# Gating stage of a streaming encoder: u of tiles 0 and 1 by seven block products for six of eight groups instead of four

## The chip, the cores and the metric

The kernel runs on one core of one Trainium2 chip. The metric is the time of one execution on the device, in microseconds (us); 2098.18 us is the median of three runs before the change. Engines are named as in the profile: PE (TensorE, matmuls), PEld (its weight loads), DVE (VectorE), ACT (ScalarE), POOL (GpSimd) and SP (SyncE, which here issues the DMAs).

## The reference

A two-layer encoder step for 1024 prompt rows and 32 sample rows of width 1024, in fp32. Layer 0 mixes by spatial gating, layer 1 by pooling; each has a squared-ReLU FFN behind it. The change concerns the gating:

```python
def sgu_mixer(h, w_in, g_v, w_s, b_s, w_out, T):
    """gMLP spatial gating: u * (W_s v + b) within chunks of T positions (T <= 128)."""
    z = jax.nn.gelu(h @ w_in)                 # (rows, 4096)
    u, v = jnp.split(z, 2, axis=-1)           # 2048 each
    v = rmsnorm(v, g_v)
    vr = v.reshape(bsz, L // T, T, SGU_GROUPS, SGU_GROUP_DIM)      # 8 groups of 256
    w = w_s[:, :T, :T] * sgu_chunk_mask()[:T, :T]
    s = jnp.einsum('gij,bnjgd->bnigd', w, vr) + b_s...
    return (u * s) @ w_out, v                 # w_out: 2048 x 1024
...
x = x + gt1 * rmsnorm(mix, g_norm[i, 1])
h = rmsnorm(x, g_norm[i, 2]) * (1 + sc2) + sh2
f = jnp.square(jax.nn.relu(h @ ffn_w_up[i])) @ ffn_w_down[i]
```

The normalised v of the sample rows is an output too (`state_sgu_sample`).

## The kernel before

Activations lie feature-major (features on partitions, rows as columns), in three tiles: tile 0 and tile 1 of 384 prompt rows, tile 2 of 256 prompt and the 32 sample rows. Every fp32 matrix is kept as a high and a low part (`wh`, `wl`, `hh`, `hl`), and a product is three matmuls: high with high, high with low, low with high (`products`, L1134 to L1136). ACT makes the high part of a weight by a copy (L592), DVE the low part by a subtraction; all wrapped DVE operations, that one too, have line L80.

**Weights** come as a list `stream` of pieces of 512 KB, written out at the start of the program. SP loads them into three `raw` buffers in the order of the list; `stream_step`, called from `weave()` between the products, consumes them in that order. `some_ada(n)` puts n pieces of the adaLN weights into the list; these are multiplied on DVE, four steps of 128x512 a piece. `fillers` are generators for other work (sums, norms, the state output) that `weave()` advances when their turn comes. A scheduler then places each engine's instructions, so the order on an engine isn't that of the code.

**The gating stage** follows the v part. Its list `mixes` names pairs of groups and the tiles they are done for. `sgu_item` does one entry for one tile in the plain form: four blocks of u (128 features each, 24 matmuls into `pu`, gelu at L1600); per group the spatial product (`spatial`, L1531, tiles `psp`) from a load `vl` of the v rows (L1499); `gate` multiplies; `split` makes `ush` and `usl`; `down` adds eight blocks `po` to the tile's sum `acc`. `upairs()` does the groups in `UPAIRS` for tiles 0 and 1 together: `pair_item` with a `gate` computes u of two blocks of features for both tiles from 2x2 blocks by seven products of 12 matmuls (`quad_product`, L1758 to L1760, into `pfau`, `pfbu`, `pfcu`) instead of eight. For this `quads` forms the weight sums (A1, S31, S24, A22) on DVE, and the filler `u_sums` the sums of activations (`usum_*`, kept in `combo_u`, `combo_acc`, `combo_r` and, for one of the four, in the place of tile 0's first half, which must no longer be needed then). Its `hook` runs the spatial products and the gating between the seven products, `place` keeps the result, and the down half is 192 matmuls (`pgu`).

Before, the entries are: groups 4 and 5 of tile 0; 6 and 7 of tile 0; then `upairs()` for groups 0 to 3 of tiles 0 and 1; groups 0, 1 and 2, 3 of tile 2; then 4, 5 and 6, 7 of tiles 1 and 2. When a tile's sum is complete, its norm and residual (`to_ffn0`: `pn_r_0x` for tile 0, `pn_rs` for tile 1) go into the fillers, and the FFN of layer 0 follows (`pf`, `pg`, and in its own pair chunks `pfa`, `pfb`).

The filler `state` (`sgu_state`, L1421 to L1440) writes the sample's normalised v in four steps: loads of `vst` (L1426) and `gvb` (L1428, a row broadcast to 32 partitions), one DVE step, a store (L1439). Its two buffers, the `vl` loads and two of the places of a pair chunk come from one pool, `x3`, with three places.

Of the kernel before, what the change touches and what calls it, by code (L numbers as in the profile page):

```python
# [35 lines left out]
def tile_stream_encoder_step(  # L36
# [99 lines left out]
    def A(t, kb, c0=0, w=None):  # L136
        w = ncol[t] - c0 if w is None else w
        return acc[t][:, kb, HALO + c0 : HALO + c0 + w]
# [5 lines left out]
    def ps_up(name):  # L144
        return psum.tile([P, 512], F32, tag="pu", bufs=2, name=name)

    def ps_dn(name):
        return psum.tile([P, 512], F32, tag="pd", bufs=3, name=name)

    def ps_ms(name):  # L150
        return psum.tile([P, 512], F32, tag="pm", bufs=3, name=name)

    def t_m(name):
        return work.tile([P, 384], F32, tag="m", bufs=3, name=name)
# [4 lines left out]
    def t_hid(kind, name, dtype=F32R):  # L159
        return work.tile([P, 384], dtype, tag="h" + kind, bufs=5, name=name)  # L160
# [185 lines left out]
    def w_groups(n):  # L346
        gs, _ = mixes[n]
        for g in gs:
            for k in range(2):
                f = 2 * g + k  # L350
                add_w(
                    ("u", n, g, k),
                    sgu_w_in[0][:, f * P : (f + 1) * P].rearrange("(k p) f -> p k f", p=P),
                    (8, P),
                )
        for q in range(2):
            for g in gs:
                add_w(
                    ("o", n, g, q),
                    sgu_w_out[0][g * 256 : (g + 1) * 256, q * 512 : (q + 1) * 512].rearrange(  # L360
                        "(k p) d -> p k d", p=P
                    ),
                    (2, 512),
                )

    def w_upair(p):
        for j in range(4):
            f = 4 * p + j
            add_w(
                ("up", ("u", p), j),  # L370
                sgu_w_in[0][:, f * P : (f + 1) * P].rearrange("(k p) f -> p k f", p=P),
                (8, P),
                ("one", "two")[j % 2],
            )
        for q in range(4):
            add_w(
                ("dn", ("u", p), q),
                sgu_w_out[0][p * 512 : (p + 1) * 512, q * 256 : (q + 1) * 256].rearrange(
                    "(j p) d -> p j d", p=P
                ),  # L380
                (4, 256),
            )
# [31 lines left out]
    every = list(range(NT))  # L414
# [5 lines left out]
    passes += [(1, c, PAIR, 1) for c in range(1, 8)]  # L420
    passes += [(1, c, [NT - 1], 2) for c in (0, 2, 4, 6)]
    LEND_AT = (("v", 1, 3), ("up", 0, 0))
    UPAIRS = (0, 1)

    rest = []

    def some_ada(n):
        for _ in range(min(n, len(rest))):
            add, l, j = rest.pop(0)
            add(l, j)  # L430
# [20 lines left out]
        some_ada(8)  # L451
    rest += [(add_wide, 1, j) for j in (*range(8, 16), *range(8), *range(16, 48))]

    mixes = [((4, 5), every[:1]), ((6, 7), every[:1]), ((0, 1), every[2:]), ((2, 3), every[2:])]
    mixes += [((4, 5), every[1:]), ((6, 7), every[1:])]
    for n in range(len(mixes)):
        w_groups(n)
        if n == 1:
            for p in UPAIRS:
                w_upair(p)  # L460
                some_ada(3)
        if n > 3:
            some_ada(5)
    for n, (l, c, tiles, m) in enumerate(passes):
        if tiles == PAIR:
            w_chunk(n, (1 if c < 3 else 2) if l else (5 if c == 1 else 6) if c < 7 else 1)
# [360 lines left out]
    def need_w(key):  # L827
        state["used"] = max(state["used"], wpos[key])
        while key not in witem:
            assert stream_ready(), key  # L830
            stream_step()
        return witem[key]
# [8 lines left out]
    def w_finish(key):  # L841
        w_free(key)
# [35 lines left out]
    def weave(streams=1):  # L878
        if streams:
            n = 0  # L880
            run_deferred()
            while n < streams and stream_ready() and not stream_waits():
                turn = bool(subs) and stream[state["next"]][0] == "wide"
                stream_step()
                n += not turn
        while time["dve"] < time["pe"] - slack[0] and fillers:
            if not pull():
                break
# [240 lines left out]
    def products(ps, n, terms, of=None):  # L1129

        i0, last = (0, len(terms) - 1) if of is None else (of[0], of[1] - 1)
        tick(3 * len(terms) * (0.004 + n / 2265.0))
        for i, (wh, wl, rh, rl) in enumerate(terms, i0):
            mm(ps[:, :n], wh, rh, start=i == 0, stop=False)  # L1134
            mm(ps[:, :n], wh, rl, start=False, stop=False)  # L1135
            mm(ps[:, :n], wl, rh, start=False, stop=i == last)  # L1136
# [100 lines left out]
    with tc.manual_schedule():  # L1237
# [63 lines left out]
        ps = ps_ms("pv0_5")  # L1301
# [105 lines left out]
    for p, b in v_order:  # L1407
        ps = ps_dn(f"pv{p}_{b}")
# [40 lines left out]
    def flush():  # L1449
        while pending:  # L1450
            pending.pop(0)()

    def split(dst_hi, dst_lo, src, n):
        act(out=dst_hi[:, :n], in_=src[:, :n], func=AF.Copy)  # L1454
        tt(out=dst_lo[:, :n], in0=src[:, :n], in1=dst_hi[:, :n].bitcast(F32), op=ALU.subtract)

    def accumulate(t, d, ps, first):
        n = ncol[t]
        if first:
            act(out=A(t, d), in_=ps[:, :n], func=AF.Copy)  # L1460
        else:
            tt(out=A(t, d), in0=A(t, d), in1=ps[:, :n], op=ALU.add)

    def up_terms(wkey, t):
        wh, wl = need_w(wkey)
        return [
            (wh[:, k * P : (k + 1) * P], wl[:, k * P : (k + 1) * P], hh[t][:, k, :], hl[t][:, k, :])
            for k in range(KB)
        ]
# [106 lines left out]
    def sgu_item(p, t, mix, after):  # L1576
        gs, tiles = mixes[p]
        last = t == tiles[-1]
        n = ncol[t]
        hid = []  # L1580

        def put(g, k, s):
            a, b = t_hid("h", f"ush{g}_{t}_{k}"), t_hid("l", f"usl{g}_{t}_{k}")
            split(a, b, s, n)
            hid.append((a, b))

        inputs, factors, spatial, gate = gating(t, mix, put)
        us = []

        def up(g, k):  # L1590
            if k == 0:
                inputs(g)
            ps = ps_up(f"pu{g}_{t}_{k}")
            products(ps, n, up_terms(("u", p, g, k), t))
            if k == 0:
                factors(g)
            if last:
                w_finish(("u", p, g, k))
            u = t_m(f"u{g}_{t}_{k}")
            act(out=u[:, :n], in_=ps[:, :n], func=AF.Gelu_apprx_tanh)  # L1600
            us.append(u)

        def down():
            for d in range(KB):
                ps = ps_dn(f"po{gs[0]}_{t}_{d}")
                terms = []
                for j, (a, b) in enumerate(hid):
                    wh, wl = need_w(("o", p, gs[j // 2], d // 4))
                    o = (j % 2) * 512 + (d % 4) * P
                    terms.append((wh[:, o : o + P], wl[:, o : o + P], a[:, :n], b[:, :n]))  # L1610
                products(ps, n, terms)
                accumulate(t, d, ps, gs[0] == (4 if t == 0 else 0))
                if d == 0 and after is not None:
                    st = Stat(t, f"rs_{t}")
                if after is not None:
                    st.square(d)
                if last and d % 4 == 3:
                    for g in gs:
                        w_finish(("o", p, g, d // 4))
                weave(d % 2)  # L1620
            if after is not None:
                after(st)

        for j in range(4):
            up(gs[j // 2], j % 2)
            if j % 2 == 1:
                gate(gs[j // 2], spatial(gs[j // 2]), us)
            weave(2 if len(tiles) == 1 else 1)
            if j == 0:
                flush()  # L1630
        pending.append(down)

    more_hid = [None, 0]
# [78 lines left out]
    def pair_item(p, after, ends, gate=None):  # L1712
# [115 lines left out]
        def down():  # L1828
            sts = {}
            for q in range(4):  # L1830
                wh, wl = need_w(("dn", p, q))
                for t in tiles:
# [5 lines left out]
                    for d, ps in two:  # L1838
                        if wait == 4:
                            products(ps, n, [term(wh, wl, t, j, d) for j in range(4)])  # L1840
                        accumulate(t, d, ps, gate is not None and c == UPAIRS[0] and t > 0)
                        if t in ends:
# [146 lines left out]
    def upair_item(p):  # L1989
# [30 lines left out]
        gate["hook"] = hook  # L2020
        pair_item(("u", p), to_ffn0, [0] if p == UPAIRS[-1] else [], gate)

    def upairs():
        u_open.append("h0")
        need_w(("up", ("u", UPAIRS[0]), 0, "A1"))
        state["kept"] = 2
        for p in UPAIRS:
            upair_item(p)
# [4 lines left out]
        acc[NT - 1] = acc_tile(NT - 1)  # L2033

    for p, (gs, tiles) in enumerate(mixes):
        if p == 2:
            upairs()
        mix = {g: sgu_group(g) for g in gs}
        for t in tiles:
            sgu_item(p, t, mix, to_ffn0 if gs[-1] == 7 and t > 0 else None)  # L2040
# [342 lines left out]
```

## Time and profile before

| | us |
|---|---|
| median of three runs (lowest, highest) | 2098.18 (2097.35, 2099.37) |
| the profiled execution: its time | 2097.82 |
| its span in the trace | 2096.0 |
| granted TensorE clock, mean | 0.999 |

Sections of the stage in the trace: groups 4 and 5 of tile 0 from 222.1, groups 6 and 7 of tile 0 from 241.8, the first pair chunk from 278.1, the second from 363.2, tile 2 from 430.8, and the FFN's first chunk is under way at 645. The first and the last products of neighbouring entries overlap, since the down half of an entry runs behind the first product of the next one. In the lines that follow, L12 is line 12 of the kernel; a line of a timeline gives start, length, engine, line, operation, out<-in, shapes and the number of instructions in it, and, in brackets, the idle time before it and what ended that.

### The profile page before, as it was taken

The numbers are of one execution on the slowest core, as the hardware profiler recorded it, in microseconds if no ns is written. First come the engines' busy times: TensorE is split into PE (matmuls) and PEld (weight loads), VectorE is DVE, ScalarE is ACT, GpSimd is POOL, SyncE is SP. The second block draws the span as 40 slices with busy tenths as digits, with TensorE's granted clock in tenths as the row PEclk, the third lists the DMA queues.
The fourth block names the chain that finished last, engine by engine and source line by source line (L and its number), as shares of the span: only waits on it lengthen the run. The fifth ranks groups of instructions, "written<-read, shape, count | busy, mean of one in ns | idle before, by whom it ended". The sixth has DMA issues, their size and how long they took to land.

```text
span 2096.0 us, 32878 instructions
## 1 busy us (share of the span) xinstructions
PE 2075.2 (99%) x12742; PEld 2004.8 (96%) x12742; DVE 1636.7 (78%) x2953; ACT 1060.3 (51%) x1902; POOL 22.3 (1%) x44
## 2 busy tenths in 40 slices
PE   8999999999999999999999999999999999999998
PEld 6878999999999999999999999999999999999998
DVE  6799786889789998888868989896867654569554
ACT  5633443454247643344446766675435443365555
POOL 0000000000000000000000000000000000001100
PEclk9999999999999999999999999999999999999999
DMA  8585534365444443343424667643223221148863
GB/s 296 164 264 181 185 109 131 116 208 181 139 128 138 131 136 111 121 131 111 131 83 141 206 195 240 192 142 98 91 76 113 84 81 59 53 125 230 204 178 93
DMA packets 410737, 303.91 MB, mean 145 GB/s; under 512 B 47022, under 2 KB 373974, under 8 KB 410580
## 3 DMA queue, kind: packets, MB, share of 16 engines
q1 hardware_dynamic: 409652, 300.52, 47.4%
q8 instruction: 100, 1.64, 0.3%
q0 software_dynamic: 896, 1.28, 0.2%
q14 instruction: 57, 0.47, 0.1%
q10 hardware_dynamic: 32, 0.01, 0.0%
HBM read 271.09 MB, written 30.66 MB: 144 GB/s over the span
## 4 chain that ended last, share of the span: by engine, by line
PE 88%; DVE 7%; DMA 2%; ACT 2%; issue 1%; SPq 0%; DVEq 0%; ACTq 0%
PE pg L1135 11%; PE pg L1134 11%; PE pg L1136 11%; PE pf L1134 4%; PE pf L1136 4%; PE pf L1135 4%; PE pfa L1758 3%; PE pfa L1760 3%; PE pfa L1759 3%; PE pv L1160 2%; PE pv L1162 2%; PE pv L1161 2%; PE po L1134 2%; PE po L1135 2%; PE po L1136 2%; PE pu L1134 2%
## 5 line engine op out<-in xcount | busy, mean ns | idle before, releaser
L1134 PE MATMUL pg<-fh,wh_dn 128*128 128x384 f32 (+1 forms) x960 | 311.4, 325 | 1.4 <-ACT fh L1454 1.0
L1135 PE MATMUL pg<-fl,wh_dn 128*128 128x384 f32 (+1 forms) x960 | 310.4, 323 | 0.1
L1136 PE MATMUL pg<-fh,wl_dn 128*128 128x384 f32 (+1 forms) x960 | 309.9, 323 | 0.0
L80 DVE TENSOR_TENSOR acc<-acc,pg 128x384 f32<-128x384 f32 (+1 forms) x272 | 143.8, 533 | 106.0 <-PE pg L1136 105.4
L80 DVE TENSOR_TENSOR wl_dn<-raw,wh_dn 128x1024 fp32r<-128x1024 f32 x136 | 166.0, 1221 | 71.2 <-ACT wh_dn L592 43.0
L80 DVE SCALAR_TENSOR_TENSOR aa<-raw,csil,aa 128x512 f32<-128x512 f32 (+1 forms) x364 | 208.4, 619 | 6.3 <-DMA raw<-in_w_ada_dram 5.8
L1134 PE MATMUL pf<-hh,wh_up 128*128 128x288 f32 (+1 forms) x632 | 192.3, 305 | 0.0
L1135 PE MATMUL pf<-hl,wh_up 128*128 128x288 f32 (+1 forms) x632 | 191.1, 302 | 0.0
L1136 PE MATMUL pf<-hh,wl_up 128*128 128x288 f32 (+1 forms) x632 | 190.8, 302 | 0.0
L1134 PEld LDWEIGHTS pg<-fh,wh_dn 128*128 128x128 f32 x960 | 180.1, 188 | 3.0 <-ACT fh L1454 1.6
L592 ACT ACTIVATE wh_dn<-raw 128x1024 fp32r<-128x1024 f32 x136 | 143.7, 1057 | 75.2 <-PE pf L1135 34.0
L1135 PEld LDWEIGHTS pg<-fl,wh_dn 128*128 128x128 f32 x960 | 180.2, 188 | 1.0 <-DVE fl L80 0.6
L1136 PEld LDWEIGHTS pg<-fh,wl_dn 128*128 128x128 f32 x960 | 180.2, 188 | 0.0
L592 ACT ACTIVATE wh_up<-raw 128x1024 fp32r<-128x1024 f32 x79 | 83.6, 1058 | 79.0 <-PE pg L1135 46.0
L1136 PEld LDWEIGHTS pf<-hh,wl_up 128*128 128x128 f32 x632 | 118.9, 188 | 0.3 <-DVE wl_up L80 0.3
L1135 PEld LDWEIGHTS pf<-hl,wh_up 128*128 128x128 f32 x632 | 118.6, 188 | 0.5
L1134 PEld LDWEIGHTS pf<-hh,wh_up 128*128 128x128 f32 x632 | 118.5, 187 | 0.6 <-ACT wh_up L592 0.2
L80 DVE TENSOR_TENSOR wl_up<-raw,wh_up 128x1024 fp32r<-128x1024 f32 x79 | 96.4, 1220 | 28.7 <-ACT wh_up L592 28.7
L1134 PE MATMUL pg<-fx,wh_dn 128*128 128x288 f32 (+1 forms) x352 | 109.4, 311 | 0.2 <-ACT fx L1454 0.2
L1764 ACT ACTIVATE a<-pfa 128x384 f32<-128x384 f32 x84 | 40.9, 487 | 133.6 <-PE pfa L1760 133.5
L1135 PE MATMUL pg<-fx,wh_dn 128*128 128x288 f32 (+1 forms) x352 | 108.3, 308 | 0.0
L1136 PE MATMUL pg<-fx,wl_dn 128*128 128x288 f32 (+1 forms) x352 | 108.0, 307 | 0.0
(825 smaller groups left out, 5675.4 us busy)
## 6 DMA issues: line engine op xcount, KB each, us to landing
raw<-in_ffn_w_up_dram SPq DMA_DIRECT2D x136, 512.0 KB, 4.0
raw<-in_ffn_w_down_dram SPq DMA_DIRECT2D x136, 512.0 KB, 4.1
raw<-in_w_ada_dram SPq DMA_DIRECT2D x90, 512.0 KB, 4.2
raw<-in_sgu_w_in_dram SPq DMA_DIRECT2D x48, 512.0 KB, 4.4
raw<-in_sgu_w_out_dram SPq DMA_DIRECT2D x32, 512.0 KB, 3.6
xd<-acc SPq DMA_DIRECT2D x8, 1536.0 KB, 8.4
xo_r<-xd SPq DMA_DIRECT2D x32, 384.0 KB, 4.5
vd<-vt SPq DMA_DIRECT2D x32, 256.0 KB, 3.8
```

Source lines behind the costliest of these rows:

```text
L80: return op(out, *args, **kw)
L592: act(out=wh, in_=r, func=AF.Copy)
L1134: mm(ps[:, :n], wh, rh, start=i == 0, stop=False)
L1135: mm(ps[:, :n], wh, rl, start=False, stop=False)
L1136: mm(ps[:, :n], wl, rh, start=False, stop=i == last)
L1160: mm(ps[:m, :], a_h, wh[:, o : o + 512], start=k == 0, stop=False)
L1161: mm(ps[:m, :], a_h, wl[:, o : o + 512], start=False, stop=False)
L1162: mm(ps[:m, :], a_l, wh[:, o : o + 512], start=False, stop=k == KB - 1)
L1758: mm(ps[:, :n], wh[:, o], rh, start=first and k == 0, stop=False, skip_group_check=True)
L1759: mm(ps[:, :n], wh[:, o], rl, start=False, stop=False, skip_group_check=True)
L1760: mm(ps[:, :n], wl[:, o], rh, start=False, stop=k == HK - 1, skip_group_check=True)
L1764: i = act(out=x, in_=ps[:, :n], func=AF.Copy)
```

## The change

A third pair chunk: `UPAIRS` gets groups 4 and 5. The entry for groups 4 and 5 of tile 0, ahead of the pair chunks, falls away, and the one for 4 and 5 of tiles 1 and 2 is left for tile 2 alone. Tile 0's sum begins with groups 6 and 7; `upairs()` comes at the second entry instead of the third; the 16 adaLN pieces of the stage stand four behind each pair chunk's weights and four in the last entry (before: three behind each of two, five in each of the last two entries).

```diff
-    UPAIRS = (0, 1)
+    UPAIRS = (0, 1, 2)
...
-    mixes = [((4, 5), every[:1]), ((6, 7), every[:1]), ((0, 1), every[2:]), ((2, 3), every[2:])]
-    mixes += [((4, 5), every[1:]), ((6, 7), every[1:])]
+    mixes = [((6, 7), every[:1])] + [((g, g + 1), every[2:]) for g in (0, 2, 4)]
+    mixes += [((6, 7), every[1:])]
     for n in range(len(mixes)):
         w_groups(n)
-        if n == 1:
+        if n == 0:
             for p in UPAIRS:
                 w_upair(p)
-                some_ada(3)
-        if n > 3:
-            some_ada(5)
+                some_ada(4)
+        if n == 4:
+            some_ada(4)
...
-                accumulate(t, d, ps, gs[0] == (4 if t == 0 else 0))
+                accumulate(t, d, ps, gs[0] == (6 if t == 0 else 0))
...
-        if p == 2:
+        if p == 1:
             upairs()
```

The instructions change places from the gating stage to the first FFN chunks; behind them the order is the same on every engine. PE has 12148 rows instead of 12172, DVE 2645 instead of 2630, SP 669 in both.

On DVE, in the first half of the first pair chunk (group 0), before; `wl_up_..._S` are low parts of weight sums, `raw` the sums, `r22u` a block of u of tile 0, `s` the gating of a spatial product:

```order
L80 TENSOR_TENSOR wl_up_('u', 0)_1_S_3099<-raw_2987,wh_up_('u', 0)_1_S_3098 128x512
L80 TENSOR_TENSOR wl_up_('u', 0)_1_S_3099<-raw_2750,wh_up_('u', 0)_1_S_3098 128x512
L80 TENSOR_TENSOR raw_2750<-raw_2987,raw_2750 128x512
L80 TENSOR_TENSOR raw_2750<-raw_2750 128x512
L80 TENSOR_TENSOR r22u_0_3079<-a3u_0_3077,b1u_0_3003 128x384
L80 TENSOR_SCALAR s_0_0_3082<-psp_0_0_3047,vec_111,bs_2807 128x384
L80 TENSOR_SCALAR s_0_1_3089<-psp_0_1_3051,vec_111,bs_2807 128x384
```

The same place after, with the first step of the state output in it (`vst`):

```order
L80 TENSOR_TENSOR wl_up_('u', 0)_1_S_2759<-raw_2412,wh_up_('u', 0)_1_S_2758 128x512
L80 TENSOR_TENSOR wl_up_('u', 0)_1_S_2759<-raw_2623,wh_up_('u', 0)_1_S_2758 128x512
L80 TENSOR_TENSOR raw_2412<-raw_2623,raw_2412 128x512
L80 TENSOR_SCALAR vst_2668<-vst_2668,rv,gvb_2670 32x512
L80 TENSOR_TENSOR r22u_0_2739<-a3u_0_2737,b1u_0_2639 128x384
L80 TENSOR_TENSOR raw_2412<-raw_2412 128x512
L80 TENSOR_SCALAR s_0_0_2742<-psp_0_0_2701,vec_111,bs_2420 128x384
L80 TENSOR_SCALAR s_0_1_2749<-psp_0_1_2705,vec_111,bs_2420 128x384
```

The state step has moved from the mix ahead of the chunk to a place in front of `r22u` and the two `s`; the other three follow further down in the same chunk.

On SP, the loads of v rows for the first pair chunk, before: `vl_0_2813` and `vl_1_2815` are those of group 0 for tiles 0 and 1, `vl_0_2709` belongs to the mix ahead, and the last store of the state output stands in front of them.

```order
L528 DMA raw_2646<-in_sgu_w_out_dram 128x2x512
L1428 DMA gvb_2590<-in_sgu_g_v_dram 32x512
L528 DMA raw_2701<-in_sgu_w_in_dram 128x8x128
L1499 DMA vl_0_2709<-vd 128x3x256
L1439 DMA out_dram<-vst_2588 32x512
L1481 DMA bs_2807<-in_sgu_b_s_dram 128x128
L1499 DMA vl_0_2813<-vd 128x3x256
L528 DMA raw_2707<-in_sgu_w_in_dram 128x8x128
L1499 DMA vl_1_2815<-vd 128x3x256
```

After, the loads of the chunk's group 1 (`vl_0_2713` for tile 0, `vl_1_2788` for tile 1) with the state output's loads and stores around them:

```order
L1428 DMA gvb_2676<-in_sgu_g_v_dram 32x512
L1426 DMA vst_2680<-vd 32x512
L528 DMA raw_2796<-in_sgu_w_out_dram 128x4x256
L1439 DMA out_dram<-vst_2674 32x512
L1428 DMA gvb_2682<-in_sgu_g_v_dram 32x512
L1481 DMA bs_3293<-in_sgu_b_s_dram 128x128
L528 DMA raw_2829<-in_sgu_w_out_dram 128x4x256
L1499 DMA vl_0_2713<-vd 128x3x256
L1439 DMA out_dram<-vst_2680 32x512
L1426 DMA vst_2719<-vd 32x512
L528 DMA raw_2914<-in_sgu_w_out_dram 128x4x256
L1428 DMA gvb_2721<-in_sgu_g_v_dram 32x512
```

The loads of group 1 now stand behind stores of the second and third state step, which wait for DVE, and share the three `x3` places with them.

## The prediction

> **What bounds the kernel now.** The page comes first: its span, and the busy share of each engine.
>
> ```profile
> span 2096.0 us, 32878 instructions
> PE 2075.2 (99%) x12742; PEld 2004.8 (96%) x12742; DVE 1636.7 (78%) x2953; ACT 1060.3 (51%) x1902; POOL 22.3 (1%) x44
> ```
>
> PE is busy for 2075.2 of 2096.0 us, so a matmul less is time gained unless it comes back as a wait of PE. Next, the waits of PE over the whole run: engine, line, tile, what ended the wait, total us, number, longest.
>
> ```profile
> PE pg L1134 <- ACT fh L1454: 1.0, 1, 1.0
> ...
> PE pn_r_0x L1005 <- ACT sc_r_0x L958: 0.9, 1, 0.9
> PE po L1135 <- DVE usl L80: 0.8, 1, 0.8
> PE pfa L1758 <- ACT a L1764: 0.7, 2, 0.5
> ...
> PE pg L1134 <- DVE acc L80: 0.4, 1, 0.4
> ```
>
> Two of these five lie in the gating stage (`po`, `pn_r_0x`), 1.7 us together, and three in the first FFN chunks behind it, 2.1 us. Then the busy time of the engines by stretches: length, then PE, PEld, DVE, ACT, POOL, the granted clock, the DMA share and GB/s. The stretches are the first mix (groups 4 and 5 of tile 0), the second (6 and 7), and the two pair chunks.
>
> ```profile
> 222.10:250.00 27.90, 27.90 (x177) 27.60 (x172) 25.79 (x64) 14.42 (x24) 0.00 (x0) 1.00 0.70 216
> 250.00:278.00 28.00, 28.00 (x172) 27.96 (x171) 17.82 (x30) 13.47 (x22) 0.00 (x0) 1.00 0.60 184
> 278.09:363.17 85.08, 85.08 (x509) 84.72 (x508) 67.69 (x126) 31.70 (x55) 0.00 (x0) 1.00 0.33 102
> 363.17:430.80 67.63, 67.63 (x408) 67.37 (x408) 54.80 (x106) 29.36 (x49) 0.62 (x2) 1.00 0.42 126
> ```
>
> PE has no gap in any of them, at the full clock. DVE has 2.1 us free in the first, 10.2 in the second, 17.4 and 12.8 in the pair chunks. So the stage is bound by PE alone, and the question is only whether the new order opens gaps.
>
> **The change, part by part.** First the matmuls. Groups 4 and 5 of tiles 0 and 1 cost 8 block products of 12 matmuls for each of two column blocks in the plain form: 2 tiles x 4 blocks x 24 = 192. As a pair chunk they cost 2 x 7 x 12 = 168. Spatial products, transposes and the down half keep their number, so 24 matmuls of 128x384 go. Their pitch comes from the PE timeline inside one such product (start, length, instruction):
>
> ```profile
> 262.89 0.33 PE L1134 MATMUL pu<-hh,wh_u 128*128 128x384 f32 x1
> ...
> 266.88 0.34 PE L1136 MATMUL pu<-hh,wl_u 128*128 128x384 f32 x1
> ```
>
> 23 intervals in 3.99 us are 0.1735 us each; 24 x 0.1735 = 4.16 us off PE. The Trainium skill ("TensorE: Matmul & The Clock Gate", section "Back-to-back issue gap") speaks against so much: it gives 81 ns per matmul at 128 columns and 131 ns at 512 in a sustained stream, and N/2.4 + 2.5 ns, 162.5 ns here, for one alone. By the sustained figures, between which 114 ns would be an estimate for 384 columns, the saving would be 2.7 us; the row stands above both, and I go by the row.
>
> Next, what the pair chunk adds on the other engines. From the groups of instructions (count, busy us, mean ns, idle before):
>
> ```profile
> L80 DVE TENSOR_TENSOR raw<-raw 128x512 f32<-128x512 f32 x64 | 44.0, 687 | 0.9
> L80 DVE TENSOR_TENSOR wl_up_S<-raw,wh_up_S 128x512 fp32r<-128x512 f32 x56 | 37.3, 686 | 37.8 <-PE pfb L1759 37.8
> L80 DVE TENSOR_TENSOR wl_u<-raw,wh_u 128x1024 fp32r<-128x1024 f32 x22 | 26.6, 1218 | 13.4 <-ACT wh_u L592 13.0 <-PE pu L1136 0.4
> L80 DVE TENSOR_TENSOR r<-a,b 128x384 f32<-128x384 f32 x28 | 15.5, 554 | 8.8 <-ACT a L1764 8.7
> L80 DVE SCALAR_TENSOR_TENSOR aa<-raw,csil,aa 128x512 f32<-128x512 f32 x196 | 139.6, 746 | 6.3 <-DMA raw<-in_w_ada_dram 5.8
> L1764 ACT ACTIVATE a2u<-pfau 128x384 f32<-128x384 f32 x4 | 2.0, 492 | 6.3 <-PE pfau L1760 3.5 <-DVE wr L80 2.8
> L1009 ACT ACT_TABLE_LOAD x4 | 5.1, 1283 | 0.1
> ```
>
> Two column blocks need 8 weight sums of 128x512 on DVE (8 x 0.687 = 5.5 us), more splitting (1.22 + 2 x 0.69 + 1.22 + 0.69 = 4.5 us for each block pair instead of 2 x 1.22, so 4.1 in all), and 6 sums of 128x384 (6 x 0.554 = 3.3): some 13 us of DVE. ACT gets 8 copies (8 x 0.492 = 3.9 us), as much in splits again, and two more table loads, since tile 0's and tile 1's norms now fall between gelus at separate places: 2 x 1.28 = 2.6 us. None of it is on the path by its sum: spread over a third pair chunk of some 68 us it is what the second one has now, 54.8 of 67.6 on DVE and 29.4 on ACT, without a gap on PE. The Trainium skill ("ScalarE: Activation LUTs", section "What ACT_TABLE_LOAD costs") puts a switch at about 2.66 us, a load of 1.283 and a drain of 1.38; by that the two cost 5.3 us of ACT instead of 2.6. The load agrees with the row, and ACT has room for either. If a table load lay in front of the norm that PE waits for, it would cost 1.3 us; the one wait there (`pn_r_0x`, 0.9) exists already and its chain is the same after.
>
> The adaLN pieces keep their number, 16, but stand 4 + 4 + 4 behind the pair chunks and 4 in the last mix, instead of 3 + 3 and 5 + 5. That puts one more piece (four DVE steps of 0.746, 3.0 us) into each down half, against 12.8 us free: nothing. In turn 6 fewer lie in the mixes just ahead of the FFN, so that part of the 2.1 us of waits there may go. The largest, on the PE timeline, with its idle time and releaser:
>
> ```profile
> 645.13 0.80 PE L1134 MATMUL pg<-fh,wh_dn 128*128 128x384 f32 x3 [0.99 <-ACT fh L1454]
> ```
>
> It is ACT that ends it, behind tile 1's norm and the weight copies, and of both some is done earlier after the change: between 0 and -2 us, and I take -0.8.
>
> Now the new order at the stage's start. There is one mix less ahead of the first pair chunk, so it starts one mix earlier: at 241.77, where before the second mix's `pu` began, instead of 278.09.
>
> ```profile
> 241.38 0.62 DVE L80 SCALAR_TENSOR_TENSOR s<-psp,vec,bs 128x384 f32<-128x384 f32 x1
> 241.77 0.42 PE L1134 MATMUL pu<-hh,wh_u 128*128 128x384 f32 x1
> ...
> 254.20 0.55 DVE L80 TENSOR_TENSOR combo_acc<-usum_y,combo_acc 128x384 fp32r<-128x384 f32 x1
> 254.67 0.73 DVE L80 SCALAR_TENSOR_TENSOR vst<-vst,rv,gvb 32x512 f32<-32x512 f32 x1
> ...
> 278.09 0.42 PE L1758 MATMUL pfau<-hh,wh_up_('u', 0)_0_A 128*128 128x384 f32 x1
> ...
> 297.11 0.33 PE L1758 MATMUL pfbu<-hh,wh_up_('u', 0)_0_S 128*128 128x384 f32 x1
> ...
> 303.50 1.50 PE L1531 MATMUL psp<-wr,vl 128*128 128x128 f32 x12
> ```
>
> *Entry.* The second product (`pfbu`) comes 297.11 - 278.09 = 19.02 us behind the chunk's start, so at 260.8 after, and the order puts 23 matmuls between it and the first use of S24's low part: 260.8 + 23 x 0.1735 = 264.8. Until then DVE has to do, from the `s` at 241.38 on, 34 steps of 128x384, 6 of 128x512, 2 of 128x1024 and two small ones (0.5 us), the activation sums among them, which before had a mix more of time. At full durations (0.554, 0.687 and 1.22) that is 18.8 + 4.1 + 2.4 + 0.5 = 25.8 us, ending at 267.2; at the pitch of back-to-back steps (254.67 - 254.20 = 0.47, and the others shorter by 0.08 likewise) 16.0 + 3.6 + 2.3 + 0.5 = 22.4, ending at 263.8. So 0 to 2.4 us of stall; most steps run at pitch, and I take 0.3.
>
> *State steps.* The filler `state` makes the sample's state output in four steps, each with two loads into the `x3` places, a step on DVE and a store. Before, all four were done ahead of the first pair chunk; after, by the order, they stand inside it, among the gating steps on DVE and between the chunk's own `vl` loads on SP.
>
> ```profile
> 260.99 0.74 DVE L80 SCALAR_TENSOR_TENSOR vst<-vst,rv,gvb 32x512 f32<-32x512 f32 x1 [2.85 <-DMA gvb<-in_sgu_g_v_dram]
> 268.45 0.73 DVE L80 SCALAR_TENSOR_TENSOR vst<-vst,rv,gvb 32x512 f32<-32x512 f32 x1
> ...
> 308.29 0.55 DVE L80 TENSOR_TENSOR r22u<-a3u,b1u 128x384 f32<-128x384 f32 x1
> 308.87 1.14 DVE L80 SCALAR_TENSOR_TENSOR s<-psp,vec,bs 128x384 f32<-128x384 f32 x2
> ...
> DMA to landing us min/median/max: 2.5/3.2/3.2
> ...
> DMA to landing us min/median/max: 2.4/4.2/6.3
> ```
>
> (The last two are the landings of `gvb` and of `vl`.) The first group's spatial products end at 241.77 + (303.50 - 278.09) + 6 x 0.1735 (six of `pfcu`'s matmuls now stand ahead of them) + 1.5 = 269.7. That frees the place for the first `gvb`: issue 0.4, landing 3.2, its step 0.7, so 274.0. Behind that step on DVE wait `r22`, a weight sum and the `s` that frees the PSUM of the tile 1 product `psp_1_1`: 0.5 + 0.6 + 0.6, so 275.7. PE comes to it, by the order 26 matmuls and half a spatial product behind 269.7, at 275.0: a stall of 0.7, between 0 (if `gvb` lands in 2.5) and 1.5.
>
> The second group's `vl` loads stand behind the second and third step on SP. The one for tile 0 I put at 282.9, landing at 287.1; PE needs it 92 matmuls, two spatial products and a transpose behind 269.7, at about 288: hidden by 0.9, and 1.2 late if it takes the longest 6.3. The one for tile 1 can go only when tile 0's spatial product has freed its place; it has 22 matmuls of cover, 3.8 us, against 2.4 to 6.3: 0 to 2.5, 0.4 with the median of 4.2. The down half starts with 40 matmuls of cover (6.9 us) instead of 48 for the last gating step: 0 to 1, I take 0.3.
>
> *Sum.* -4.16 + 0.3 + 0.7 + 0.4 + 0.3 - 0.8 = -3.3; I allow 0.4 for landings in the second and third pair chunk and say -2.9. The profiled execution took 2097.8 us (span 2096.0 and 1.8 around it), 0.4 under the median of 2098.2, so against the median: **2095.3**. The ends: everything free and all FFN waits gone gives -4.2 - 2.0, 2092.0; all stalls at their upper ends (2.4 + 1.5 + 1.2 + 2.5 + 1 = 8.6, less 4.2) gives +4.4, 2102.6.
>
> **The rivals.** *All hidden.* No stall at the entry and from the state steps, and the FFN waits shrink: 2098.2 - 4.2 - 1 to 2 = 2092 to 2093. For it: PE has no gap in any stretch of the stage, and the second pair chunk shows a chunk in steady state without one. Against: the 0.7 of the first state step follows from the order.
>
> *The state steps hold DVE.* DVE works in order, so a step that stands at its head for a `gvb` holds everything behind it: weight splits, `s`, gelu's products. One row shows such a hold, 2.85 us at 260.99, at a place where PE had cover. If each of the four steps holds DVE so long inside the chunk and PE has 0.7 us of cover at each, that is 4 x 2.15 = 8.6 us, and with the 0.7 of the two loads and the down half together 9.3; less 4.16, +5.1, **2103.3, slower**. The gain is lost where the holds pass 1.6 us each (4 x (1.6 - 0.7) + 0.7 = 4.3), and the loss can be told where they pass 2.6. For it: each `gvb` waits for the store of a step before it, so a late step makes the next late. Against: before the chunk DVE was hardly held (2.85 once in four), and by my walk the later three are held 0 to 1 us.
>
> *The gain is eaten.* Stalls of about 4 us, from the entry (2.4) and the tile 1 loads (two at 1 to 2.5), leave 2098: no change.
>
> **How the numbers follow.** A measurement of this kernel can tell about 0.2%, 4.2 us, from no change. Chances: the forecast 0.45, the gain eaten 0.15, all hidden 0.24, the state steps or something of the kind 0.16. All hidden lies about 5 to 6 us below and counts as faster, with a part of the forecast's own spread (2093 to 2098; 0.02 below 2094): faster 0.26. The forecast's rest and the eaten gain are within: 0.58. Slower 0.16. The range leaves out most of the slow rival and the last of the hidden one: 2092.0 to 2101.5.
>
> **What would show it.** In the changed profile: PE with 24 fewer matmuls; the first `pfau` at about 241.8; `psp_1_1` of the first group with an idle of about 0.7 us behind DVE's `s`; the second group's `psp` of tile 1 with 0 to 1 us behind the DMA of `vl`; S24 with under 1 us behind DVE; `pn_r_0x` as it is; the FFN rows `pg<-fh` and `pfa` smaller. I am wrong if PE shows waits of more than 4 us between 240 and 310, if the third pair chunk has gaps of its own, or if a wait of more than 2 us turns up behind the stage, where the order is the same.

## The result, and the profile after

Over 22 runs of each the changed kernel took 2101.09 us in the median (2097.88 to 2106.14), the kernel before 2098.43 (2097.35 to 2101.23): a ratio of 1.0012 with a 95% interval of 1.0007 to 1.0018. It is slower by some 2.7 us, where 2.9 us less was forecast. Its runs spread more than those of before, and they spread with the granted clock: the mean span was 2096.8 us in 4 runs at a mean clock of 0.999, 2098.2 in 10 at 0.998 and 2101.6 in 8 at 0.997. So even the executions at the best clock show nothing of the 4.2 us: the kernel before had a span of 2096.0 us in its profile. The profiled execution took 2106.14 us; it is one of the eight, the slowest of the 22, and shows the loss at its largest.

The page of the changed kernel first, the span and the busy times:

```profile
span 2103.5 us, 32876 instructions
PE 2075.0 (99%) x12718; PEld 2003.0 (95%) x12718; DVE 1647.8 (78%) x2973; ACT 1069.7 (51%) x1918; POOL 22.3 (1%) x44
```

There are 24 matmuls fewer, as worked out, and DVE has 11.1 us more, where some 13 were worked out; but PE's busy time has not fallen by 4.2 us: somewhere its matmuls took longer. The waits of PE over the whole run, in the columns of before:

```profile
...
PE ada L710 <- DVE part L696: 2.1, 2, 1.8
PE psp L1531 <- DVE wr L80: 1.9, 2, 1.6
...
PE po L1134 <- ACT ush L1454: 1.2, 1, 1.2
PE pn_r_0x L1005 <- ACT sc_r_0x L958: 1.2, 1, 1.2
PE pfa L1758 <- ACT a L1764: 1.1, 2, 0.8
...
PE pg L1135 <- DVE combo_R L80: 0.9, 2, 0.5
PE pu L1134 <- ACT u L1600: 0.9, 1, 0.9
PE pn_rp L1005 <- ACT sx_rp L958: 0.8, 1, 0.8
PE pgu L1134 <- DVE s L80: 0.7, 1, 0.7
...
PE pgu L1134 <- ACT fxu L1454: 0.3, 1, 0.3
```

The waits at the first pair chunk (`pgu`) are small. A new one stands out, `psp <- wr`, and its place is tile 2's first entry. PE's timeline there, with the idle time before each row in brackets:

```profile
478.28 0.29 PE L1134 MATMUL pu<-hh,wh_u 128*128 128x288 f32 x1
478.41 0.29 PE L1135 MATMUL pu<-hl,wh_u 128*128 128x288 f32 x1
...
480.15 0.29 PE L1136 MATMUL pu<-hh,wl_u 128*128 128x288 f32 x1
482.03 0.71 PE L1531 MATMUL psp<-wr,vl 128*128 128x128 f32 x4 [1.59 <-DVE wr L80]
...
484.48 0.61 PE L1134 MATMUL pu<-hh,wh_u 128*128 128x288 f32 x1 [0.92 <-ACT u L1600]
484.89 0.44 PE L1135 MATMUL pu<-hl,wh_u 128*128 128x288 f32 x1
485.13 0.44 PE L1136 MATMUL pu<-hh,wl_u 128*128 128x288 f32 x1
```

From 484.48 on the matmuls stand 0.24 us apart; at 478.28 they stood 0.13 apart. The stretches around it say why (the granted clock is the third figure from the end):

```profile
480.00:483.90 3.90, 1.97 (x16) 1.62 (x14) 2.23 (x6) 0.83 (x1) 0.00 (x0) 0.99 0.91 236
483.90:490.80 6.90, 6.32 (x26) 6.30 (x27) 4.57 (x9) 2.56 (x6) 0.00 (x0) 0.51 0.60 188
490.80:500.00 9.20, 9.20 (x70) 9.05 (x69) 6.84 (x14) 8.45 (x15) 0.00 (x0) 1.00 0.38 138
```

After 3.9 us in which PE was idle for 1.93, the clock was halved for 6.8 us. The 27 matmuls from 484.48 to the first `po` took 6.5 us; the same 27 took 3.7 us before. So it cost 2.8 us.

Adding up all of PE's gaps over 0.2 us in the two timelines gives the account of the profiled execution: 1.0 us against 0 up to 440 us, 5.3 against 1.7 from there to 620, 2.1 against 2.0 at the FFN's start, 4.4 against 0.8 behind 740, and 2.8 for the half clock. That is +11.1; less the 4.2 of the 24 matmuls, +6.9, and the spans differ by 7.5; 0.6 us of it are not accounted for.

What `wr` waited for is in DVE's timeline of the same place:

```profile
478.16 1.22 DVE L80 TENSOR_TENSOR wl_u<-raw,wh_u 128x1024 fp32r<-128x1024 f32 x1
479.30 0.28 DVE L1486 COPY wt<-wsT 128x128 f32<-128x128 f32 x1
479.88 0.46 DVE L80 TENSOR_TENSOR usl<-s,ush 128x288 fp32r<-128x288 f32 x1 [0.31 <-ACT ush L1454]
480.41 0.11 DVE L1487 MEMSET wt<- 64x64 f32 x1
480.55 1.23 DVE L80 TENSOR_TENSOR wl_u<-raw,wh_u 128x1024 fp32r<-128x1024 f32 x1
481.70 0.63 DVE L80 TENSOR_SCALAR wr<-wt,rv 128x128 f32<-128x128 f32 x3
```

The six DVE rows run almost without a gap and `wr` is the last: it stands behind two low parts of weights (`wl_u`). DVE came here late. In the half chunk ahead, the third pair chunk's down half, it had hardly any time left; the stretches are the last half chunk of before and that of after:

```profile
397.00:430.80 33.80, 33.80 (x197) 33.77 (x196) 30.97 (x57) 12.38 (x20) 0.00 (x0) 1.00 0.49 146
```

```profile
429.50:463.20 33.70, 33.70 (x197) 33.54 (x197) 32.79 (x57) 10.88 (x18) 0.31 (x1) 1.00 0.51 154
```

DVE was busy for 30.97 of 33.8 us before and for 32.79 of 33.7 after. (The second stretch begins some 2 us earlier in its half chunk than the first; from 431.20 to 465.10 DVE is busy for 32.97 of 33.9.) The groups of DVE instructions in the same two stretches show the difference: 10 steps of the adaLN pieces in the first, 14 in the second.

```profile
L80 DVE SCALAR_TENSOR_TENSOR aa<-raw,csil,aa 128x512 f32<-128x512 f32 x10 | 6.9, 746 | 0.0
```

```profile
L80 DVE SCALAR_TENSOR_TENSOR aa<-raw,csil,aa 128x512 f32<-128x512 f32 x14 | 9.6, 746 | 0.0
```

Those are the four steps of the one piece that the change put there. The weight pieces for tile 2 wait for a `raw` buffer behind them: on SP's timeline the issue of the first four took 9.1 us before and 14.2 after, and the fourth went out 20.7 us behind the half's first `pgu` matmul before (418.9 against 398.2) and 25.6 after (458.2 against 432.6).

```profile
410.19 9.06 SPq L528 DMA_DIRECT2D raw<-in_sgu_w_in_dram  x4
```

```profile
444.34 14.24 SPq L528 DMA_DIRECT2D raw<-in_sgu_w_in_dram  x4
```

### The profile page after: what moved, and what is told of

Same layout as the page of the kernel before. It is cut to its first block, busy times and chain, and to the rows that moved or that the text cites. A ratio compares the mean times of both kernels' runs of the same rounds, so it can differ in the third digit from the quotient of the medians.

```text
span 2103.5 us, 32876 instructions
## 1 busy us (share of the span) xinstructions
PE 2075.0 (99%) x12718; PEld 2003.0 (95%) x12718; DVE 1647.8 (78%) x2973; ACT 1069.7 (51%) x1918; POOL 22.3 (1%) x44
## 3 DMA queue, kind: packets, MB, share of 16 engines
q8 instruction: 99, 1.62, 0.3%
## 4 chain that ended last, share of the span: by engine, by line
PE 86%; DVE 7%; DMA 3%; ACT 2%; issue 1%; SPq 0%; DVEq 0%; ACTq 0%
PE pg L1134 11%; PE pg L1135 11%; PE pg L1136 11%; PE pf L1134 4%; PE pf L1136 4%; PE pf L1135 4%; PE pfa L1758 3%; PE pfa L1760 3%; PE pfa L1759 3%; PE pv L1160 2%; PE pv L1162 2%; PE pv L1161 2%; PE pfb L1758 1%; PE pfb L1759 1%; PE pfb L1760 1%; PE pgu L1134 1%
```

## The experiments

Ratios are to the kernel before, run on the same chip, with 95% intervals. Its own median was 2100.0 to 2100.8 us there, against 2098.43 above, so an expected time in us is read here as a ratio to 2098.43. All but three variants start from the changed kernel. Theory A: tile 2's weights come late because of the adaLN piece ahead of them. Theory B: the state steps in the first pair chunk cost the time. Theory C: the pair chunk's own work does, wherever the pieces stand.

**Pieces 3 + 3 + 3 and 7 in the last entry.**

```diff
-                some_ada(4)
+                some_ada((3, 3, 3)[p])
         if n == 4:
-            some_ada(4)
+            some_ada(7)
```

> The changed kernel with the adaLN pieces spread 3 + 3 + 3 behind the pair chunks and 7 in the last entry (instead of 4 + 4 + 4 and 4). Theory A (the weight stream comes late to tile 2's first entry, because one adaLN piece more stands ahead of it; PE then waits there 1.6 and 0.9 us, and the clock is halved for 6.8 us): the wait for wr shrinks to under 1 us, no stretch at half clock, median about 2098.0. Theory B (the state steps inside the first pair chunk cost the time): unchanged, about 2101. Theory C (the third pair chunk's own work on DVE and ACT makes the lateness, the adaLN pieces matter little): 2100 to 2101, with the wait for wr still over 1.2 us.

Measured: 1.0023 (1.0014 to 1.0032), worse than the change itself. All three theories missed the time. At the first entry A was right: what was left is a wait for `usl`, 0.8 us, as before the change. But a wait for `wr` of 2.1 us came at 544 us, in tile 2's third entry, with half clock behind it; and with three pieces more in the last entry there were 2.4 us of gaps at the FFN's start and one of 1.8 at 774 us, which halved the clock again; so did one of 1.9 at 1040 us, for an adaLN fold (`ada <- part`).

**Pieces 4 + 4 + 0 and 8 in the last entry.** The same lines with (4, 4, 0) and 8.

> The changed kernel with the adaLN pieces 4 + 4 + 0 behind the pair chunks and 8 in the last entry: none between the third pair chunk's weights and those of tile 2. Theory A: no wait over 0.8 us at tile 2's first entry, no half clock in the stage, median 2096 to 2097.5. Theory B: about 2101. Theory C: 2099.5 to 2101.

Measured: 1.0057 (1.0044 to 1.0069). The waits of PE between 440 and 740 us:

```profile
PE pf L1134 <- ACT hh L1094: 4.4, 1, 4.4
PE pu L1134 <- ACT u L1600: 2.0, 1, 2.0
PE po L1134 <- ACT ush L1454: 1.5, 1, 1.5
PE pn_r_1x L1005 <- ACT sc_r_1x L958: 1.5, 1, 1.5
PE pn_r_1x L1005 <- DVE sm_r_1x L80: 1.1, 1, 1.1
...
PE psp L1531 <- DVE wr L80: 0.2, 1, 0.2
```

`psp <- wr` is down to 0.2 and the clock was full from 222 to 663 us, as A said; but the 1.5 us for `po` lie in tile 2's first entry too, where A allowed 0.8. And the pieces cost more where they went, behind tile 1's residual: 7 us ahead of the FFN. All three theories missed the time again.

**State output at the last entry.**

```diff
-    fillers.append(("state", sgu_state()))
...
         if p == 1:
             upairs()
+        if p == 4:
+            fillers.append(("state", sgu_state()))
```

> The changed kernel with the filler of the state output appended only at the last entry, so that its four steps stand behind tile 2's groups and none in a pair chunk. Theory A: the first pair chunk's waits (0.7 and 0.3 us) go, the waits at tile 2's entry and the half clock in some of the runs stay: about 2100. Theory B: 2097 or less. Theory C: as A.

Measured: 0.9998 (0.9990 to 1.0007). The waits in the pair chunks fell from 1.0 to 0.3 us, as A and C said. In the profile PE waited 1.1 us for `wr` at 480 us, and the clock stayed full there. Tile 2's fourth weight piece was as late as in the change (25.6 us behind the first `pgu`). The profiled execution, the fastest of the 11, has a span of 2093.8 us, 2.2 below that of before, so the matmuls saved can show where the clock holds; over all runs it comes out even. For the time the run doesn't decide between the theories: A's 2100 is a ratio of 1.0007, B's 2097 one of 0.9993, and the interval holds both. With the pieces left where they were, moving the state steps took the ratio from 1.0012 to 0.9998, so their place bears on the loss as well.

**The kernel before with 4 + 4 and 4 + 4 pieces.**

```diff
-                some_ada(3)
+                some_ada(4)
         if n > 3:
-            some_ada(5)
+            some_ada(4)
```

> The kernel before with its adaLN pieces 4 + 4 behind the two pair chunks and 4 + 4 in the last two entries (instead of 3 + 3 and 5 + 5). Theory A: two pieces more ahead of tile 2's weights make PE wait at tile 2's first entry by over 1.5 us, with half clock in some runs: 2100 to 2103. Theories B and C: as before, 2098 to 2099.

Measured: 0.9989 (0.9980 to 0.9998), faster. A `wr` wait of 1.1 us does come at tile 2's first entry, but it and the wait for tile 0's norm in the second are 2.3 us together, where two waits made 1.7 before; no half clock follows, and the FFN's start has 0.6 instead of 2.0. So A's mechanism exists without the third pair chunk, its size here was wrong (B and C, too, had forecast more), and placing the pieces alone gains 1.1 per mille without it.

Theory D then was that DVE is full in the whole stage, so that a piece must leave it; E, that only the pieces ahead of tile 2 matter. The next four have 12 pieces in the stage, the other four going to the FFN of layer 1: (4, 4, 4) and 0; (4, 4, 0) and 4; the latter with the state output late; and the kernel before with 4 + 4 and 2 + 2.

> The changed kernel with 4 + 4 + 4 adaLN pieces behind the pair chunks and none in the last entry; the four pieces move to the FFN of layer 1 (12 in the stage instead of 16). Theory D (the DVE work of the third pair chunk fills the stage: whatever DVE work stands late in it turns into waits of PE, at tile 2's first entry or at the FFN's start, and pairs of such waits halve the clock): the waits at tile 2's first entry stay (wr, about 1 to 1.6 us), those behind 540 us shrink to under 2 us together; ratio to the kernel before 0.999 to 1.001. Theory E (only the pieces ahead of tile 2 matter): no better than the changed kernel, 1.001.

> The changed kernel with 4 + 4 + 0 pieces behind the pair chunks and 4 in the last entry (12 in the stage): no piece between the third pair chunk's weights and tile 2's, and no more than the changed kernel has in the last entry. Theory D: no wait for wr at tile 2's first entry, FFN start as in the changed kernel, ratio 0.997 to 0.999. Theory E: the same.

> As the run with 4 + 4 + 0 + 4 pieces, and the state output's filler appended only at the last entry. If the 1.0 us of waits in the first pair chunk come from the state steps, and nothing late takes their place: 1 us below that run, ratio 0.9965 to 0.9985. If the state steps, now at the last entry, meet a full DVE there: equal to it or above.

> The kernel before with 4 + 4 pieces behind its two pair chunks and 2 + 2 in its last two entries (12 in the stage): what moving four pieces out of the stage is worth without the third pair chunk. Theory D: little, since before DVE has room: 0.9985 to 0.9995, as with 4 + 4 + 4 + 4. If the pieces as such cost time in the stage: 0.997.

Measured: 1.0003 (0.9994 to 1.0012), 1.0004 (0.9995 to 1.0012), 1.0002 (0.9993 to 1.0011), and 0.9986 (0.9977 to 0.9995) for the kernel before. The first lies in D's range, the second above both theories', the third beside the second, as its other case had it, and the last in D's range at its lower edge. Whether fewer pieces help isn't shown: the first three lie below the change's 1.0012, but their intervals reach it, and 0.9986 can't be told from the 0.9989 with 16 pieces. With 4 + 4 + 0 + 4 the wait for `wr` is 0.5 us, but `pu <- u` comes with 2.1 at the next entry and halves the clock; with the state output late it is 1.5, halves it too, and a `po` of 1.6 stands ahead of it. The lateness moves on.

Theory D' narrowed it to single halves: one adaLN piece too many in a down half or in the last entry makes the weights behind it late. Theory G: three entries of tile 2 alone in a row (two before) want weights faster than the stream brings them. The pieces are 3 + 3 + 3 and 3; then also with this order (tile 2's norm moves with its last entry), then with the state output late instead, and the change itself again:

```diff
-    mixes = [((6, 7), every[:1])] + [((g, g + 1), every[2:]) for g in (0, 2, 4)]
-    mixes += [((6, 7), every[1:])]
+    mixes = [((6, 7), every[:1])] + [((g, g + 1), every[2:]) for g in (0, 2)]
+    mixes += [((6, 7), every[1:]), ((4, 5), every[2:])]
```

> The changed kernel with 3 + 3 + 3 adaLN pieces behind the pair chunks and 3 in the last entry (12 in the stage, the other four in the FFN of layer 1). Theory D' (the third pair chunk's down half had 2.8 us of DVE left, not 12.8; the fourth piece fills it and makes tile 2's weights late; a piece too many in the last entry does the same at the FFN's start): first entry's waits as before the change, about 0.8 us, last entry and FFN start under 2 us, ratio to the kernel before 0.998 to 0.9995. Theory G (tile 2 alone for three entries in a row, one more than before, wants more weights for each us of PE than the stream brings, whatever the pieces): waits of 1 us and more in tile 2's second and third entry, ratio 1.0000 to 1.0010.

> As the run with 3 + 3 + 3 + 3 pieces, and groups 4 and 5 of tile 2 after groups 6 and 7 of tiles 1 and 2 instead of before them, so that only two entries in a row have tile 2 alone, as before the change. Theory G: the waits in tile 2's second and third entry go, 1.5 to 3 us below that run. Theory D': the same as that run within 1 us.

> As the run with 3 + 3 + 3 + 3 pieces, and the state output's filler appended only at the last entry. The waits of 1.0 us in the first pair chunk go to 0.3 or 0.4; 0.5 to 1 us below that run if nothing late takes their place.

> The changed kernel itself once more, on the chip of the three runs above. Ratio to the kernel before 1.0007 to 1.0018 as measured already. Its profile tells which waits come in each execution and which by chance: by theories D' and G those between 480 and 550 us come again, within 0.5 us each, and the wait of 1.8 us at 1037 us, behind a piece that landed late, doesn't.

Measured: 0.9994 (0.9985 to 1.0003); 1.0024 (1.0014 to 1.0033); 0.9988 (0.9980 to 0.9997); 1.0014 (1.0004 to 1.0024). With 3 + 3 + 3 + 3 DVE was busy for 31.5 of 33.7 us in the third down half, and no `wr` wait came at the first entry, as D' said, and its time lies in the range of D'. Tile 2's fourth weight piece went out 21.4 us behind the first `pgu`, nearly as early as in the kernel before (20.7). But one of 1.7 came at 543 us, in the third entry of tile 2, where G looks for it. In the new order the same group waits only 0.3, as G said, but `pf` at the FFN's start waited 2.9 us for the low part of a weight and `pfa` 2.4, both followed by half clock. So G holds at its place and not for the time. The state output late is worth 1.8 us here (2097.83 against 2099.67 in the means of 11 runs each), more than the 0.5 to 1 expected from the waits in the first pair chunk; with 4 + 4 + 0 + 4 it was worth 0.4 (2100.41 against 2100.83).

The change again shows which waits belong to it. PE's timeline and the stretch behind it:

```profile
483.88 1.23 PE L1531 MATMUL psp<-wr,vl 128*128 128x128 f32 x4 [2.36 <-DVE wr L80]
```

```profile
483.90:490.30 6.40, 6.40 (x28) 6.40 (x29) 4.84 (x11) 3.16 (x5) 0.00 (x0) 0.50 0.68 207
```

The wait for `wr` and the half clock come at the same place in a second execution, the wait 0.8 us longer than in the first, where 0.5 was allowed; the wait for `u` behind it didn't come again. The wait for the fold at 1037 us came too, against my expectation, with 1.5 us.

**Both groups turned at the entry's start**, so that `wr` no longer stands behind the two weight splits; for the change, for 3 + 3 + 3 + 3 with the state output late, and for the kernel before with 4 + 4 + 2 + 2:

```diff
             if k == 0:
                 factors(g)
+                for x in gs:
+                    while mix[x][2]:
+                        mix[x][2].pop()()
```

> The changed kernel with the spatial weights of both groups of an entry turned (transpose, copy, masking) at the entry's first block instead of each at its own group; wr of the second group then stands on DVE ahead of the two weight splits that it waited behind. If that wait and the half clock that follows it are the loss: no wait for wr at 480 to 485 us, no half clock there, ratio to the kernel before 0.9985 to 1.0000. If the lateness of the weights only moves on (to pu or po, a product later): 1.0005 to 1.0015 as without the edit.

> Three pair chunks with 3 + 3 + 3 + 3 adaLN pieces, the state output at the last entry and both groups turned at the entry's start: the waits of 1.4 us (wr, 541 us) go, 1 to 1.5 us below the same without the turn: ratio 0.9980 to 0.9985. If it moves on: 0.9988 as without.

> Two pair chunks (the kernel before) with 4 + 4 + 2 + 2 pieces and both groups turned at the entry's start: 0.9982 to 0.9986 (0.7 us of wr wait less at most than without the turn). The third pair chunk is worth its 24 matmuls only if the run above lies more than 1 us below this one.

Measured: 1.0006 (0.9997 to 1.0015); 0.9988 (0.9979 to 0.9997); 0.9988 (0.9979 to 0.9997). In the change alone, the waits of PE between 440 and 620 us are now:

```profile
PE pu L1134 <- ACT u L1603: 1.6, 1, 1.6
PE po L1134 <- ACT ush L1454: 0.9, 1, 0.9
PE po L1135 <- DVE usl L80: 0.8, 1, 0.8
PE wsT L1485 <- DMA wt<-in_sgu_w_s_dram: 0.4, 1, 0.4
```

No `wr`, no half clock in the stage, 3.5 us instead of 5.3. The intervals overlap those of the change (1.0014 and 1.0012), so the time alone doesn't prove the difference; the profile does for the wait and the half clock. The rest moved on to `po` and `pu`, and 1.0006 lies in the range given for that case; at 1034 us the fold's wait was 2.6 us and halved the clock there. With the other two, the turn gained nothing over the same without it. And the best with three pair chunks, 2097.14 us, equals the best with two, 2096.97 (and 0.9986 without the turn): with the best placing found for each, the third is worth nothing that can be measured. Five versions beat the kernel before, by 1.1 to 1.4 per mille: three with two pair chunks and 4 + 4 pieces behind them, and two with three pair chunks, 3 + 3 + 3 + 3 pieces and the state output late.

## Why the prediction was wrong

The direction was wrong. That 2101.1 lies inside the range, at its upper end, is luck: the range reached so far for stalls at the chunk's entry and its loads, and the time was lost elsewhere. By its steps:

- *24 matmuls, 4.16 us*: right. The account comes within 0.6 us with 4.2, and where the clock held (the profile with the state output late) the span fell by 2.2 with 1.5 us of new waits between 440 and 620.
- *Entry, state steps, loads and down half, 1.7 us*: right in size as waits, 1.0 and 1.6 us in the two profiles. The place was off: `pgu` waits for the last gating steps, 0.7 and 0.3, and `psp_1_1` 0.2 at most. But moving the state steps away gained 0.4 us in one pair of runs, 1.8 in another, and took the change from 1.0012 to 0.9998, so their cost isn't only those waits.
- *One adaLN piece more in each down half, "against 12.8 us free: nothing"*: this step failed. 12.8 us was the free time of a whole pair chunk; the down half, where the piece stands, had 33.8 - 30.97 = 2.8, and the piece takes 9.6 - 6.9 = 2.7 by the rows above. It cost no wait in the down half itself, but behind it, through the three `raw` buffers: tile 2's fourth piece went out 4.9 us later, and between 440 and 620 us PE waited 3.6 us more than before. With three pieces there the weights were early again and the `wr` wait at the first entry was gone; with four in the kernel before it came up, 1.1 us. How much of the loss in time is this step's isn't settled, since with the piece moved the waits came elsewhere.
- *The clock*: left out of the sum. A wait was priced at its length; this one cost 2.8 us more in the first profiled execution of the change, where the clock was halved behind it, and 3.0 in the second (39 matmuls from the `psp` to the first `po` in 8.05 us, before in 5.0).
- *FFN waits, -0.8*: 2.1 and 1.3 us against 2.0, so +0.1 and -0.7. (Of the 2.1 us counted there before, 0.2 lie at 1513 us, far behind.) The kernel before with 4 + 4 and 4 + 4 pieces came to 0.6, by its pieces and without the third pair chunk.
- *The same order behind the stage, so nothing there*: wrong by 3.6 us in both profiles, most of it at `ada <- part` (1.8 and 1.5) and around 1606 to 1608 us (1.2 and 1.5). With the state output late there were under 2 us there instead of 4.4, in one profile.

Of the rivals, "the gain is eaten" (2098) and "the state steps hold DVE" (2103.3) lie on either side of 2101.1. The first had its stalls in the wrong places. The second had the direction right, but not the mechanism: PE's waits inside the chunk were 1.0 us and not the 9.3 it summed up.

What stays open: how moving the state steps gains more than the waits it removes in the pair chunk; and why the same adaLN piece, issued at about 1020 to 1025 us, lands after 5.0 to 6.2 us in the change and with the turn, and after 3.8 to 3.9 us in the kernel before, with the state output late and in the kernel before with 4 + 4 and 4 + 4, though the order around it is the same. How much of the loss tile 2 alone for three entries makes by itself was not settled either: its wait could be moved away, but not without others in its place.

## What to carry to other kernels

Read the free time of an engine in the stretch where a step is put, not in the stage: half a chunk later the same engine may be full, and its lateness shows as waits of other tiles behind it. Work that feeds PE through a small ring of buffers has to be followed to the next stage's first products. And a short wait of PE can cost more than its length, so a change that trades matmuls for waits has to count what the clock may add.

## What the runs showed of the hardware

In these 17 profiles PE's clock was halved, between 222 and 2080 us, for 3.41 us or for twice that at a time. It followed all seven waits of more than 2.0 us (2.07 to 4.43), some of those between 1.4 and 2.0, and none that was shorter and stood alone.

Which of them is told by a grid. In each profile all stretches between two changes of the clock are whole multiples of 3.413 us (139, 2 and 471 of them in the change). If PE's time is cut at that grid, 12 windows at full clock have 1.63 us of idle time or more, and half clock follows all of them; of the others, over 9000 with 1.62 or less, it follows none. The two nearest to the limit, each with the window behind it, are from 4 + 4 + 0 + 8 and from 4 + 4 + 0 + 4 with the state output late (PE's busy time is the second figure):

```profile
1042.18:1045.60 3.42, 1.79 (x17) 1.43 (x17) 3.42 (x7) 0.97 (x2) 0.00 (x0) 1.00 0.37 136
1045.60:1049.01 3.41, 3.41 (x13) 3.41 (x12) 3.27 (x9) 2.88 (x6) 0.00 (x0) 0.50 0.86 272
```

```profile
484.68:488.09 3.41, 1.79 (x12) 1.34 (x10) 1.70 (x3) 3.39 (x6) 0.00 (x0) 1.00 0.48 145
488.09:491.50 3.41, 3.20 (x20) 2.74 (x21) 2.81 (x7) 3.33 (x7) 0.00 (x0) 1.00 0.49 168
```

So the wait of 1.59 us in the change was enough with the first 0.27 us of the next one, in the window from 480.41 to 483.83, and those of 1.76 and 1.96 us elsewhere were not, since the grid cut them in two (1.57 and 1.55 us in the larger part). The halving lasted a second window where PE had idled in the first one too (0.4 to 3.2 us, four times), and one window where it hadn't (eight times).

The Trainium skill ("TensorE: Matmul & The Clock Gate", section "What's actually happening") gives windows of about 3.4 us, which agrees with the lengths; its advice against idle gaps of over about 3 us (section "Why this matters for your kernels") is looser than these runs, where one of 1.63 us did it.
